# Turning normalised tokens by transposing transfers instead of float32 transposes on TensorE

## The chip, the cores and the metric

The kernel runs on one core of a Trainium2 chip. The metric is device time of one execution in microseconds (us); the kernel before takes 2276.16 us, the median of three runs (2273.22 to 2279.15).

## The reference

Two layers of a mixer over 2048 latent tokens and 256 context tokens, 1024 features each, float32. Cut to what matters here:

```python
h  = _rmsnorm(x, norm_g) * (1.0 + scale[:, None]) + shift[:, None]     # latents, modulated by c
hc = _rmsnorm(xc, norm_g) * (1.0 + scale_c) + shift_c                  # context, modulated by c_ctx
parts = _split_cols(h @ w_in)          # q, k, v, gates, and inputs of four mixers: 2816 columns
# Fourier mixing, attention over context + latents, short convolution, pooling, each gated by silu(z)
out = jnp.concatenate([o_f, o_att, o_c, o_p], axis=-1) @ w_out
x_new = x + gate[:, None] * out        # the context is updated likewise, in the first layer only
```

So each token's row is normalised, each feature multiplied by one factor and shifted by another, and the result is multiplied by the input weights.

## The kernel before, in words

Tokens are cut into five blocks (`BLK`): the context of 256 tokens and four latent blocks of 512; a tile is 128 tokens. The products with `w_in` need the tokens with features on the partitions. They are kept as a sum of two float16 numbers, so one block is four (context: two) tiles `h` of 4 KB per partition, and each product is done in three passes (`PASSES`).

`prep` (line 234) makes them, tile by tile, as a generator: it loads a tile of x token-major (one token per partition; the next tile's load is issued first), takes the sum of squares by a Square on ScalarE (L251, its elements go to a scratch), makes the scale from it on GpSimd (`rms_scale`, L230 and L231), and scales on ScalarE (L253); it yields; then it turns the tile by eight float32 transposes on TensorE (L261), applies factor and shift on VectorE from PSUM, where both are one number per partition (L265), casts to the high half on ScalarE (L268) and subtracts to the low half on GpSimd (L269).

`token_groups` (line 344) holds the products that come out token-major: per block two `fourier_in` (`tok_pair`, L329), one `keys` and one `values` (`tok_major`, L319) and two `queries` (L329). In layer 0 (lines 1147 to 1174) the preparation of the next block takes one step ahead of each group of the current block. In layer 1 (lines 1248 to 1266) two blocks are prepared first, among steps of the output projection of the last two blocks of layer 0 (`late`, L1125), and from then on preparation runs two blocks ahead, the context last. Feature-major groups (`feat_major`, L307) follow.

`big` hands out 26 shared buffers of 4 KB per partition: modulation weights, `h`, attention keys and values, output weights. `TagPool` holds buffers that a stage owns; `TOKEN` and the numbers beside it say how many. A scheduler places the instructions of each engine in a fixed order at build time, early in the program first; every engine then runs its own queue in order and waits on semaphores. Stores and most loads are on SP's queue, loads of `prep` on SP's for the first two blocks of layer 0 and otherwise on ScalarE's. `affine` (line 196) makes factor and shift with features on the partitions; `set_gate` (line 1080) spreads such a vector along the free axis over all partitions: a diagonal on VectorE, then a product with ones.

Of the kernel before, what the change touches and what calls it, by code (L numbers as in the profile page):

```python
# [10 lines left out]
F32 = mybir.dt.float32  # L11
F32R = mybir.dt.float32r
F16 = mybir.dt.float16
BF16 = mybir.dt.bfloat16
ACTF = mybir.ActivationFunctionType
ALU = mybir.AluOpType
# [4 lines left out]
D = 1024  # L21
KC = 8
# [4 lines left out]
BLK = [(0, 256)] + [(256 + 512 * i, 512) for i in range(4)]  # L27
# [15 lines left out]
def hybrid_kernel(ctx: ExitStack, tc: tile.TileContext, T, out):  # L43
    nc = tc.nc
    PE, ACT, DVE, POOL, SP = nc.tensor, nc.scalar, nc.vector, nc.gpsimd, nc.sync
# [9 lines left out]
    sm = pool("sm", 3)  # L55
# [15 lines left out]
    def big(shape, dt, name):  # L71
        return slot.tile(shape, dt, tag="s", name=name)
# [13 lines left out]
    id32 = const.tile([128, 128], F32, name="id32")  # L86
# [107 lines left out]
    aff = {}  # L194
# [23 lines left out]
    def alloc_h(b):  # L218
        n = BLK[b][1]
        per = 2048 // n  # L220
        hT[b] = [[big([128, per, n], F16, f"h{b}{part}{i}") for i in range(KC // per)] for part in range(2)]

    def h_ap(b, part, k, t0, n, nk=1):
        per = 2048 // BLK[b][1]
        t = hT[b][part][k // per]
        return t[:, k % per, t0:t0 + n] if nk == 1 else t[:, k % per:k % per + nk, t0:t0 + n]

    def rms_scale(ss, n, count, tag):
        ms = sm.tile([128, 8], F32, tag=tag, name=tag)[:, 0:n]
        POOL.tensor_scalar(out=ms, in0=ss, scalar1=1.0 / count, scalar2=EPS, op0=ALU.mult, op1=ALU.add)  # L230
        POOL.tensor_tensor(out=ms, in0=ms, in1=nh[:, 0:n], op=ALU.pow)  # L231
        return ms

    def prep(L, b, tp, psum):

        s = 1 if b == 0 else 0
        g0, n = BLK[b]

        def load(t):
            xt = tp.tile([128, D], F32, tag="x", name="xt")  # L240
            (SP if L == 0 and b < 2 else ACT).dma_start(out=xt, in_=source(L, g0 + t * 128))
            return xt

        ahead = load(0)
        for t in range(n // 128):
            xt = ahead
            if (t + 1) * 128 < n:
                ahead = load(t + 1)
            xn = tp.tile([128, D], F32, tag="xn", name="xn")
            ss = sm.tile([128, 1], F32, tag="ss", name="ss")  # L250
            ACT.activation(out=xn, in_=xt, func=ACTF.Square, accum_out=ss)  # L251
            rstd = rms_scale(ss, 1, D, "rx")
            ACT.activation(out=xn, in_=xt, func=ACTF.Copy, scale=rstd)  # L253
            yield
            if t == 0:
                alloc_h(b)
            for half in range(2):
                pt = psum()
                for j in range(4):
                    k = 4 * half + j  # L260
                    PE.transpose(out=pt[:, j * 128:(j + 1) * 128], in_=xn[:, k * 128:(k + 1) * 128], identity=id32)  # L261
                h32 = tp.tile([128, 4, 128], F32, tag="h32", name="h32")
                for j in range(4):
                    k = 4 * half + j
                    DVE.tensor_scalar(out=h32[:, j, :], in0=pt[:, j * 128:(j + 1) * 128], scalar1=aff[L][0][:, 0, k, s:s + 1],  # L265
                                      scalar2=aff[L][0][:, 1, k, s:s + 1], op0=ALU.mult, op1=ALU.add)
                hi = h_ap(b, 0, 4 * half, t * 128, 128, 4)
                ACT.copy(out=hi, in_=h32)  # L268
                POOL.tensor_tensor(out=h_ap(b, 1, 4 * half, t * 128, 128, 4), in0=h32, in1=hi, op=ALU.subtract)  # L269
# [821 lines left out]
    def source(L, tok):  # L1091

        if L > 0:
            return xd[tok:tok + 128]
        return T["ctx"][tok:tok + 128] if tok < NCTX else T["x"][tok - NCTX:tok - NCTX + 128]
# [50 lines left out]

    gate_w = {}
    with ExitStack() as st:
        tp = TagPool(st, tc, "s0", {**TOKEN, "x": 4, "xn": 2, "h32": 2, "row": 1})
        ws = []  # L1150
        ahead = prep(0, 0, tp, aux_bank)
        for c in range(4):
            for i, _ in enumerate(modulate(0, c, aux_bank, tp, True)):
                if (c, i) == (0, 3):
                    steps(ahead, 1)
                if (c, i) == (2, 3):
                    ws += [load_w(0, *TOKEN_W[0])]
        SP.dma_start(out=gain, in_=T["gains"].partition_broadcast(128))
        ws += [load_w(0, *TOKEN_W[1])]
        SP.dma_start(out=edge, in_=T["k_edge"])  # L1160
        SP.dma_start(out=invw, in_=T["k_invw"])
        SP.dma_start(out=cd, in_=T["k_cd"])
        affine(0)
        for w in ws:
            unscale(0, w[1])
        steps(ahead, 9)
        block = token_groups(0, tp, ws)
        for b in range(5):
            ahead = prep(0, b + 1, tp, aux_bank) if b + 1 < 5 else iter(())
            if b == 4:  # L1170
                gate_w[0] = load_w(0, *GATE_W[0:2], True)
            for _ in block(b):
                steps(ahead, 1)
            steps(ahead, 9)
# [26 lines left out]
    for L in range(DEPTH):  # L1201
# [37 lines left out]
        with ExitStack() as st:  # L1239
            tp = TagPool(st, tc, f"p{L}", {"mix": 1, "ml": 2, "ot": 1, "gate": 1, "x": 2})  # L1240
            project_setup(L, kvs)
            steps(att, 12)
            fill = project(L, early, tp)
            spread(att, fill, sum(72 if b else 11 for b in blocks[-2:]) - 12, sum(BLK[b][1] // 16 for b in early), 1)
            steps(fill, 1 << 30)
            steps(att, 1 << 30)
            right.close()
            late = project(L, blocks[-2:], tp)
            if L + 1 < DEPTH:
                with ExitStack() as st2:  # L1250
                    sp = TagPool(st2, tc, f"s{L + 1}", {**TOKEN, "s": 2, "x": 2, "xn": 1, "h32": 2}, "right")
                    with tc.issue_after(load_mark[0]):
                        block = token_groups(L + 1, sp, [])
                    for b in blocks[0:2]:
                        for _ in prep(L + 1, b, sp, mx_bank):
                            steps(late, 3)
                    for i, b in enumerate(blocks):
                        ahead = prep(L + 1, blocks[i + 2], sp, mx_bank) if i + 2 < 5 else iter(())
                        if i == 4:
                            gate_w[L + 1] = load_w(L + 1, *GATE_W[0:2], True)  # L1260
                        for _ in block(b):
                            steps(ahead, 1)
                            steps(late, 8)
                        steps(ahead, 9)
                        if i == 0:
                            steps(late, 1 << 30)
            steps(late, 1 << 30)
# [98 lines left out]
```

## Time and profile before

| | |
|---|---|
| median of three runs | 2276.16 us |
| the profiled execution, its own time | 2273.57 us |
| its span | 2271.8 us |
| TensorE busy | 2158.7 us, 95% |
| VectorE busy | 1407.4 us, 62% |
| ScalarE busy | 1227.9 us, 54% |
| GpSimd busy | 936.1 us, 41% |
| share of the chain that ended last on TensorE | 68% |
| transposes of `prep` (L261) | 288, first at 31.4, last at 1303.5 us |

The page cuts the span into 40 slices of 57 us; TensorE is at nine tenths or more in nearly all. Transposes of `prep` stand in slices 1 to 3 (layer 0) and 21 to 23 (layer 1) alone. A busy share is an average over a stretch; a wait is read from the timeline, where a line gives the start, the length, the engine, the program line, and in brackets the idle time before it and what ended it.

### The profile page before, as it was taken

The numbers are of one execution on the slowest core, as the hardware profiler recorded it, in microseconds if no ns is written. First come the engines' busy times: TensorE is split into PE (matmuls) and PEld (weight loads), VectorE is DVE, ScalarE is ACT, GpSimd is POOL, SyncE is SP. The second block draws the span as 40 slices with busy tenths as digits, with TensorE's granted clock in tenths as the row PEclk, the third lists the DMA queues.
The fourth block names the chain that finished last, engine by engine and source line by source line (L and its number), as shares of the span: only waits on it lengthen the run. The fifth ranks groups of instructions, "written<-read, shape, count | busy, mean of one in ns | idle before, by whom it ended". The sixth has DMA issues, their size and how long they took to land.

```text
span 2271.8 us, 41300 instructions
## 1 busy us (share of the span) xinstructions
PE 2158.7 (95%) x16327; PEld 1292.0 (57%) x16327; DVE 1407.4 (62%) x2639; ACT 1227.9 (54%) x2297; POOL 936.1 (41%) x996
## 2 busy tenths in 40 slices
PE   7999899989998999999999989999999999899999
PEld 3997556545555555545557984554454555455554
DVE  3655886366768767666465545413567776787743
ACT  4653454346777766544445624323467766566640
POOL 2786542215454455422125862011344556333320
PEclk9999999999999999999999999999999999999999
DMA  8424455510322110223474424323124210222133
GB/s 317 145 92 129 151 178 171 182 53 26 113 76 81 54 31 28 95 79 114 141 237 134 136 76 137 112 104 103 35 70 141 70 37 31 65 74 72 61 117 121
DMA packets 164081, 237.97 MB, mean 105 GB/s; under 512 B 28618, under 2 KB 113966, under 8 KB 163886
## 3 DMA queue, kind: packets, MB, share of 16 engines
q1 hardware_dynamic: 141294, 205.95, 27.2%
q10 hardware_dynamic: 22592, 29.37, 4.2%
q8 instruction: 128, 2.10, 0.4%
q14 instruction: 67, 0.55, 0.1%
HBM read 165.94 MB, written 69.34 MB: 104 GB/s over the span
## 4 chain that ended last, share of the span: by engine, by line
PE 68%; DVE 9%; ACT 4%; POOL 4%; issue 3%; DMA 2%; SPq 0%; POOLq 0%; DVEq 0%; ACTq 0%
PE fl L307 19%; PE fl L1125 15%; PE st L307 6%; PE pv L967 4%; PE st L972 4%; PE st L973 4%; PE mx L931 4%; DVE mp L932 2%; PE pv L965 2%; PE pv L329 1%; PE st L329 1%; PE mx L853 1%; DVE pl L979 1%; POOL pl L979 1%; PE mx L683 1%
## 5 line engine op out<-in xcount | busy, mean ns | idle before, releaser
L979 POOL TENSOR_TENSOR pl<-p,ph 128x512 f16<-128x512 f32 (+1 forms) x292 | 361.8, 1239 | 577.6 <-ACT p L978 515.1
L307 PE MATMUL fl<-h,w 128*128 128x512 f16 (+1 forms) x2592 | 582.1, 370 | 12.6 <-ACT w L147 9.3
L307 PEld LDWEIGHTS <-w 128*128 128x128 f16 x3456 | 331.5, 99 | 373.1 <-issue 22.2
L977 ACT ACTIVATE ph<-st 128x512 f16<-128x512 f32 (+1 forms) x584 | 350.9, 601 | 223.0 <-PE st L973 214.7
L932 DVE TENSOR_REDUCE mp<-mx 128x1 f32<-128x512 f32 (+1 forms) x648 | 388.8, 626 | 123.3 <-PE mx L931 112.7
L1125 PE MATMUL fl<-wo,ml 128*128 128x512 f16 x1632 | 376.8, 379 | 2.5 <-DVE ml L148 2.5
L978 ACT ACTIVATE p<-st 128x512 f32<-128x512 f32 (+1 forms) x584 | 351.2, 601 | 29.7 <-DVE pl L979 20.2
L979 DVE TENSOR_TENSOR pl<-p,ph 128x512 f16<-128x512 f32 (+1 forms) x292 | 231.9, 794 | 124.3 <-ACT p L978 100.0
L1125 PEld LDWEIGHTS <-ml 128*128 128x128 f16 x1632 | 157.4, 98 | 182.1 <-DVE ml L148 3.7
L967 PE MATMUL pv<-V,ph 128*128 128x130 f16 x2320 | 230.0, 221 | 6.9 <-ACT ph L977 6.2
L967 PEld LDWEIGHTS <-ph 128*128 128x128 f16 x2320 | 170.4, 98 | 116.4 <-ACT ph L977 29.1
L931 PE MATMUL mx<-kst,qhh 128*128 128x512 f16 x512 | 191.3, 385 | 22.9 <-DVE mp L932 22.1
L972 PE MATMUL st<-qhh,kst 128*128 128x512 f16 x512 | 195.6, 382 | 7.1 <-ACT p L978 6.2
L973 PE MATMUL st<-qlm,k 65*128 65x512 f16 x512 | 196.8, 384 | 0.0
L307 PE MATMUL st<-h,w 128*128 128x512 f16 (+1 forms) x864 | 189.1, 369 | 0.0
L965 PE MATMUL pv<-V,pl 128*128 128x66 f16 x2320 | 173.0, 194 | 12.5 <-DVE pl L979 6.0
L329 PEld LDWEIGHTS <-h 128*128 128x128 f16 x1632 | 160.0, 98 | 19.9 <-POOL h L269 1.1
L965 PEld LDWEIGHTS <-pl 128*128 128x128 f16 x2320 | 134.3, 98 | 65.0 <-POOL pl L979 14.0
L319 PEld LDWEIGHTS <-h 128*128 128x128 f16 x1728 | 99.5, 98 | 1.4 <-issue 0.6
L931 PEld LDWEIGHTS <-qhh 128*128 128x128 f16 x648 | 62.5, 99 | 65.8 <-issue 25.5
L329 PE MATMUL pv<-w,h 128*128 128x256 f16 x816 | 95.0, 275 | 0.9 <-POOL h L269 0.9
L329 PE MATMUL st<-w,h 128*128 128x256 f16 x816 | 92.7, 273 | 0.0
(303 smaller groups left out, 2903.7 us busy)
## 6 DMA issues: line engine op xcount, KB each, us to landing
wm<-in_w_mod_dram SPq DMA_DIRECT2D x48, 512.0 KB, 4.7
wst<-in_w_in_dram SPq DMA_DIRECT2D x44, 512.0 KB, 5.0
mix<-mixd SPq DMA_DIRECT2D x34, 512.0 KB, 4.0
zd<-z SPq DMA_DIRECT2D x64, 256.0 KB, 2.2
wst<-in_w_out_dram SPq DMA_DIRECT2D x32, 512.0 KB, 4.3
xt<-in_x_dram SPq DMA_DIRECT2D x20, 512.0 KB, 4.7
xd<-xt SPq DMA_DIRECT2D x18, 512.0 KB, 2.8
xt<-xd ACTq DMA_DIRECT2D x18, 512.0 KB, 3.7
```

Source lines behind the costliest of these rows:

```text
L307: PE.matmul(out=ps, lhsT=w[:, wp, k, :], rhs=h_ap(b, hp, k, 0, n), start=(k == 0 and i == 0), stop=(k == KC - 1 and i == 2))
L329: PE.matmul(out=ps[:, t], lhsT=h_ap(b, hp, k, (2 * i + t) * 128, 128), rhs=w[:, :, wp, k, :], start=(k == 0 and j == 0), stop=(k == KC - 1 ...
L931: mark[0] = PE.matmul(out=ps, lhsT=qhh[:, t * 128:(t + 1) * 128], rhs=kk, start=True, stop=True).ins
L932: DVE.tensor_reduce(out=mp[:, t, i:i + 1], in_=ps, axis=AX.X, op=ALU.max)
L965: PE.matmul(out=pv[t // 2][:, t % 2, 0:66], lhsT=p, rhs=v[:, 0:66], start=False, stop=(kt == nk - 1), skip_group_check=True)
L967: PE.matmul(out=pv[t // 2][:, t % 2, :], lhsT=p, rhs=v, start=(kt == 0 and t % 2 == 0), stop=False, skip_group_check=True)
L972: mark[0] = PE.matmul(out=ps, lhsT=self.k_tile(0, kt), rhs=qhh, start=True, stop=False).ins
L973: PE.matmul(out=ps, lhsT=self.k_tile(1, kt)[0:65, :], rhs=qlm[0:65, :], start=False, stop=True)
L977: ACT.activation(out=ph, in_=ps, func=ACTF.Exp, scale=1.0 / LOGIT)
L978: ACT.activation(out=p32, in_=ps, func=ACTF.Exp, scale=1.0 / LOGIT)
L979: (POOL if kt % 2 == 0 else DVE).tensor_tensor(out=pl, in0=p32, in1=ph, op=ALU.subtract)
L1125: PE.matmul(out=ps, lhsT=ml[:, mp, k, :], rhs=wo[k][:, wp, half * 512:(half + 1) * 512], start=(k == 0 and j == 0), stop=(k == KC - 1 and ...
```

## The change

For every block but the context of layer 0, `prep` hands over to a new generator. Factor and shift are spread along the free axis once for each layer and stream (`affine_rows`: two diagonals, four float32 products with ones, four copies, into shared buffers). A tile then stays token-major: Square into a float16 pair used as scratch, scale, one VectorE operation (times the token's scale, times the row of factors), one GpSimd addition (the row of shifts), one cast on ScalarE to the high half, one subtraction on VectorE to the low half; and each half is turned by transposing transfers on SP's queue straight into `h`, four per latent tile and two per context tile. The loads of layer 0's first latent block go to ScalarE's queue. The pair (`hl`) gets two buffers in each layer; in layer 1 it takes the place of `xn` and `h32`.

```diff
+    def affine_rows(L, s, psum):
+
+        for a in range(2):
+            dg = big([128, 8, 128], F32, "dg")
+            DVE.tensor_tensor(out=dg, in0=id32.unsqueeze(1).to_broadcast([128, 8, 128]),
+                              in1=aff[L][0][:, a, :, s].unsqueeze(2).to_broadcast([128, 8, 128]), op=ALU.mult)
+            r = big([128, 1024], F32, f"row{a}")
+            for half in range(2):
+                pg = psum()
+                PE.matmul(out=pg, lhsT=ones, rhs=dg[:, 4 * half:4 * half + 4, :].rearrange("p j f -> p (j f)"), start=True, stop=True)
+                ACT.copy(out=r[:, half * 512:(half + 1) * 512], in_=pg)
+            rows[a] = r
+
+    def prep_rows(L, b, tp, psum):
+
+        g0, n = BLK[b]
+        if b < 2:
+            affine_rows(L, 1 if b == 0 else 0, psum)
+
+        def load(t):
+            xt = tp.tile([128, D], F32, tag="x", name="xt")
+            ACT.dma_start(out=xt, in_=source(L, g0 + t * 128))
+            return xt
+
+        ahead = load(0)
+        for t in range(n // 128):
+            xt = ahead
+            if (t + 1) * 128 < n:
+                ahead = load(t + 1)
+            hl = tp.tile([128, 2, D], F16, tag="hl", name="hl")
+            ss = sm.tile([128, 1], F32, tag="ss", name="ss")
+            ACT.activation(out=hl.rearrange("p a f -> p (a f)").bitcast(F32), in_=xt, func=ACTF.Square, accum_out=ss)
+            rstd = rms_scale(ss, 1, D, "rx")
+            yield
+            if t == 0:
+                alloc_h(b)
+            DVE.scalar_tensor_tensor(out=xt, in0=xt, scalar=rstd, in1=rows[0], op0=ALU.mult, op1=ALU.mult)
+            POOL.tensor_tensor(out=xt, in0=xt, in1=rows[1], op=ALU.add)
+            ACT.copy(out=hl[:, 0], in_=xt)
+            DVE.tensor_tensor(out=hl[:, 1], in0=xt, in1=hl[:, 0], op=ALU.subtract)
+            per = 2048 // n
+            for part in range(2):
+                for i in range(KC // per):
+                    SP.dma_start_transpose(out=h_ap(b, part, per * i, t * 128, 128, per), in_=hl[:, part, per * 128 * i:per * 128 * (i + 1)])
+
     def prep(L, b, tp, psum):
 
+        if (L, b) != (0, 0):
+            yield from prep_rows(L, b, tp, psum)
+            return
...
-        tp = TagPool(st, tc, "s0", {**TOKEN, "x": 4, "xn": 2, "h32": 2, "row": 1})
+        tp = TagPool(st, tc, "s0", {**TOKEN, "x": 4, "xn": 2, "h32": 2, "hl": 2, "row": 1})
...
-                    sp = TagPool(st2, tc, f"s{L + 1}", {**TOKEN, "s": 2, "x": 2, "xn": 1, "h32": 2}, "right")
+                    sp = TagPool(st2, tc, f"s{L + 1}", {**TOKEN, "s": 2, "x": 2, "hl": 2}, "right")
```

## Rows read from the trace of the kernel before

**Rows 1.** Busy time by stretch: length, then busy us (instructions) per engine, clock, DMA

```profile
60.00:206.70 146.70, 146.70 (x1743) 137.41 (x1741) 81.56 (x193) 81.11 (x136) 114.69 (x140) 1.00 0.35 115
1225.00:1350.30 125.30, 124.96 (x1508) 117.03 (x1506) 70.18 (x174) 63.38 (x108) 99.02 (x118) 1.00 0.36 113
```

**Rows 2.** Timeline of TensorE in layer 1: start us, length us, line, operation

```profile
1188.92 1.88 PE L1087 MATMUL fl<-dg,ones 128*128 128x512 f32 x4
1190.64 0.67 PE L319 MATMUL pv<-w,h 128*128 128x128 f16 x9
...
1200.53 1.04 PE L261 MATMUL mx<-id,xn 128*128 128x128 f32 x8
1201.40 4.91 PE L1125 MATMUL fl<-wo,ml 128*128 128x512 f16 x22
```

**Rows 3.** Timeline, single moments of both token stages, several engines

```profile
41.02 0.23 DVE L212 TENSOR_SCALAR ab<-modT,sh 128x16 f32<-128x16 f32 x1
...
175.03 5.40 PE L329 MATMUL pv<-w,h 128*128 128x256 f16 x48
180.27 5.40 PE L329 MATMUL st<-w,h 128*128 128x256 f16 x48
...
206.71 0.28 PE L120 MATMUL mx<-sq,ones 128*128 128x2 f32 x2
...
1157.32 1.06 ACT L251 ACTIVATE xn<-xt 128x1024 f32<-128x1024 f32 x1 [3.17 <-PE mx L1015]
...
1352.99 2.84 PE L319 MATMUL st<-w,h 128*128 128x128 f16 x48
1355.67 0.34 PE L120 MATMUL mx<-sq,ones 128*128 128x2 f32 x2
```

**Rows 4.** Groups of instructions by line, whole span: count, busy us, mean ns, idle before

```profile
L174 DVE SCALAR_TENSOR_TENSOR acc<-wm,sc,acc 128x512 f32<-128x512 f32 x56 | 57.9, 1034 | 0.8
L979 DVE TENSOR_TENSOR pl<-p,ph 128x512 f16<-128x512 f32 (+1 forms) x292 | 231.9, 794 | 124.3 <-ACT p L978 100.0 <-PE pv L965 8.8 <-issue 6.2
L251 ACT ACTIVATE xn<-xt 128x1024 f32<-128x1024 f32 x36 | 38.0, 1056 | 48.3 <-PE mx L261 34.7 <-DMA xt<-in_ctx_dram 7.5 <-PE mx L1015 3.2
L251 ACT ACTIVATION_READ_ACCUMULATOR xn<-xt 128x1 f32 x36 | 6.8, 189 | 0.0
L231 POOL TENSOR_TENSOR rx<-rx,nh 128x1 f32<-128x1 f32 x36 | 21.2, 588 | 2.1
L230 POOL TENSOR_SCALAR rx<-ss 128x1 f32<-128x1 f32 x36 | 11.9, 330 | 51.3 <-ACT xn L251 49.9
L843 POOL TENSOR_TENSOR y<-y,zf 128x1024 f32<-128x1024 f32 x8 | 19.7, 2480 | 110.0 <-DVE y L832 110.0
L446 ACT CAST qo<-q 128x1024 f16<-128x1024 f32 x17 | 17.7, 1042 | 14.1 <-DVE q L426 13.2 <-DMA qd<-qo 1.0
L1082 DVE TENSOR_TENSOR dg<-id,modT 128x1024 f32<-128x1024 f32 x3 | 3.6, 1212 | 0.0
```

**Rows 5.** DMA issues (count, size, median us to landing), and one issue on SP's timeline

```profile
mix<-mixd SPq DMA_DIRECT2D x34, 512.0 KB, 4.0
gain<-in_gains_dram SPq DMA_DIRECT2D x1, 256.0 KB, 9.6
kd<-ko SPq DMA_DIRECT2D x2, 128.0 KB, 3.1
...
111.56 0.36 SPq L448 DMA_DIRECT2D qd<-qo  x1
```

**Rows 6.** Timeline: a quiet pair on VectorE early, then GpSimd and VectorE in layer 1

```profile
32.23 2.48 DVE L148 SCALAR_TENSOR_TENSOR w<-wst,ws,w 128x1024 f16<-128x1024 f32 x2 [0.58 <-ACT w L147]
...
1360.26 0.51 POOL L413 TENSOR_SCALAR rq<-rq,winv 128x4 f32<-128x4 f32 x2
...
1364.11 3.40 DVE L148 SCALAR_TENSOR_TENSOR w<-wst,ws,w 128x1024 f16<-128x1024 f32 x2 [0.95 <-ACT w L147]
...
1365.20 1.24 POOL L413 TENSOR_SCALAR rq<-rq,winv 128x4 f32<-128x4 f32 x1
```

More of the change, by code (lines that the diff above doesn't have):

```diff
@@ L232, in rms_scale @@
         return ms
+    rows = {}
+    def affine_rows(L, s, psum):
[37 more added lines that the diff above has]
+                    SP.dma_start_transpose(out=h_ap(b, part, per * i, t * 128, 128, per), in_=hl[:, part, per * 128 * i:per * 128 * (i + 1)])
     def prep(L, b, tp, psum):
+        if (L, b) != (0, 0):
+            yield from prep_rows(L, b, tp, psum)
+            return
         s = 1 if b == 0 else 0
@@ L240, in load @@
             xt = tp.tile([128, D], F32, tag="x", name="xt")
-            (SP if L == 0 and b < 2 else ACT).dma_start(out=xt, in_=source(L, g0 + t * 128))
+            SP.dma_start(out=xt, in_=source(L, g0 + t * 128))
             return xt
```

## The prediction

> **What bounds the kernel now.** I read the page's slices first: TensorE stands at nine tenths nearly everywhere. So the question is what TensorE does in the two stretches where normalised tokens are prepared, and what stands second there. The busy times by stretch answer that [rows 1]: from 60 us to the end of layer 0's token groups TensorE is busy for all 146.7 us of 146.7, GpSimd for 114.7 (78%), VectorE and ScalarE for 81 each (55%); in the later part of layer 1's token groups TensorE has 125.0 of 125.3 us, GpSimd 99.0 (79%). [...] So TensorE sets the pace, and a microsecond taken from it is worth a microsecond only as long as nothing else needs more than it leaves. The timeline gives the pace: the last block of layer 0, which prepares no tokens beside it, runs from 175.03 to 206.71, 31.7 us [rows 3]; a block that also turns four tiles of tokens needs 4 x 0.87 us more, 35.2 us.
>
> **What is taken from TensorE.** Eight float32 transposes of a tile stand in the queue for 0.87 us (1200.53 to 1201.40) [rows 2]. The change takes them from 34 of the 36 tiles (16 in layer 0, 18 in layer 1; the two context tiles of layer 0 keep the old way): 29.6 us.
>
> **What is put on TensorE.** The factors now vary along the free axis, so each stream needs two rows spread over all partitions: four float32 products of 512 columns, as the output gate already makes; two of those take 1.72 us (1188.92 to 1190.64) [rows 2], 0.86 each. Three sets (layer 0's latents, layer 1's latents and context): 12 x 0.86 = 10.3 us. Net on TensorE: 19.3 us less (10.5 in layer 0, 8.8 in layer 1). This is the largest gain the change can give.
>
> **What moves on the other engines, per tile** [rows 4]. ScalarE loses the scaled copy and gets one cast of 1.04 us for two half-size ones; it was 55% busy, and this is worth nothing by itself. VectorE loses eight small operations that read PSUM and gets two wide ones that read SBUF twice. The first, a scalar and two tensors over 1024 columns, lies between 1.24 us (half of the 2.48 us that the like weight split takes in quiet places, beside the 3.40 us for two in [rows 6]) and 2.07 us (twice the 1.03 us of the 512-wide accumulation); I take 1.5, near the weight split, which has the same width. The second, float32 minus float16 into float16, is twice 0.79 us: 1.6. GpSimd loses two subtractions and gets one addition of 1024 columns; the product of that shape takes 2.48 us: 2.5. The sums per tile change little. What changes is that these steps stand in a row. The diagonals (6 x 1.21 us on VectorE) and the row copies (12 on ScalarE of 512 columns, some 0.7 us each, between half and the whole of the 1.04 us of the cast twice as wide) come at the heads of the stages. The loads of block 1 move from SP's queue to ScalarE's, at about 0.35 us each on ScalarE: nothing, while its cover, ScalarE's idle half, lasts.
>
> **The transposing transfers.** No row shows one. Each tile has four of 128 KB on SP (two of 256 KB for a context tile). The lower bound is a plain transfer of 128 KB, issue to issue 0.36 us and 3.1 us to landing [rows 5]: 3 x 0.36 + 3.1 = 4.2 us for the four. The upper end is the slowest landing that the issue table shows, 9.6 us, with the four one after the other: 38 us. I take 6.5 us, 3 x 1.1 + 3.1, nearest to the mix load: it moves 1024 runs of 512 bytes in 4.0 us [rows 5], and a transposing transfer reads 512 runs of half that length, so about 1.1 us apart. Queued behind them on SP are the stores of u, keys and queries and the rope and weight loads; ScalarE's evacuations wait for those stores' buffers, and TensorE for ScalarE.
>
> [...]
>
> **Where a new wait arises.** The float16 pair (tag hl) has two buffers, and one is held from the Square, which scribbles into it, until its transfers have landed. Held time: Square 1.06 + 0.19, scale 0.33 + 0.59, multiply 1.5, add 2.5, cast 1.04, subtract 1.6, transfers 6.5, together 15.3 us [rows 4, 5]; plus six hand-overs to engines that are 55 to 79% busy with operations of about 1.2 us, at half an operation each: 3.9 us, an estimate. That is 19.2 us, and with two buffers one tile per 9.6 us. TensorE without transposes uses up a tile in 31.7 / 4 = 7.9 us. So the buffers, not TensorE, set the pace, and the wait sits in ScalarE's queue, ahead of PSUM evacuations. (Before, the like buffer came free when TensorE had turned the tile, a few microseconds after the Square.)
>
> Layer 0: the factors exist at 41.25 [rows 3]. One diagonal, two products and a copy bring the first row at 44.9, and the second at 46.6; then add, cast, subtract, transfers (2.5 + 1.04 + 1.6 + 6.5) and 3.4 of hand-overs: the first tile of block 1 lands at 61.7. The sixteenth lands 15 x 9.6 = 144 us later, at 205.7, and behind it block 4 still has its second u half, keys, values and queries, 26.4 us (180.27 to 206.71) [rows 3]: 232.1 against 206.7, a loss of 25.4 us.
>
> Layer 1: the first Square starts at 1157.3 [rows 3]; first tile at 1176.5, sixteenth at 1320.5, then 26.4 us and the context's keys and values (2 x 2.7): 1352.3 against the end at 1355.7 [rows 3], a gain of 3.4 us. Here preparation runs two blocks ahead and the rest of the output projection covers the slow start; TensorE alone would allow 1355.7 - 8.8 = 1346.9. The two x buffers, held until the subtraction now (4.0 us of load, like the mix load, and about 12 of chain), allow one tile per 8 us and don't bind first.
>
> The sum: +25.4 - 3.4 = +22 us on the profiled execution's own 2273.57 us, 2295.6; that execution lies 2.6 us under the median of the three runs, so 2298 on the median's scale.
>
> **The rivals.** (1) *All is hidden*: the held time stays under 15.8 us (hand-overs near nothing and transfers near the lower bound), TensorE keeps the pace, and the whole 19.3 us come: 2257. For it: layer 1 has slack, and the schedule can pull later work forward into gaps. Against it: the bare steps with the lower bound are already 13.0 us, and layer 0 prepares just one block ahead. (2) *Balance*: held time 16.8, a tile per 8.4 us: layer 0 loses 7.4 us (61.7 + 126 + 26.4 = 214.1), layer 1 gains its 8.8: 2275, no change.
>
> (3) *VectorE and GpSimd get in each other's way.* Where the weight split ran on VectorE, two for 3.40 us, a GpSimd operation that takes 0.26 us (two for 0.51) took 1.24 [rows 6]. The old preparation's VectorE work read PSUM; the new reads SBUF twice, beside GpSimd at 78%. If each of the two waits for a GpSimd operation and the addition for one of VectorE's, about 1 us each, the held time is 22.2 and the pace 11.1 us: layer 0 ends at 61.7 + 166.5 + 26.4 = 254.6 (+47.9), layer 1 at 1157.3 + 22.2 + 166.5 + 31.8 = 1377.8 (+22.1): 2346. This decides once the held time exceeds 19.2. [...]
>
> (4) *The transfers run in series* at 3.1 us each, 12.4 for the four: held 25.1, pace 12.6; layer 0 ends at 67.6 + 189 + 26.4 = 283.0 (+76.3), layer 1 at 1157.3 + 25.1 + 189 + 31.8 = 1403.2 (+47.5): 2400. The decisive point is whether one transfer's landing holds back the next. [...]
>
> **How the numbers follow.** Forecast 0.31 (2298), hidden 0.20 (2257), balance 0.12 (2275), interference 0.22 (2346), series 0.15 (2400). A measurement of this kernel tells 0.3%, 7 us, from no change; so faster 0.20, same 0.12, slower 0.68. The range runs from the hidden case with a few microseconds below it to the series case, 2253 to 2400; beyond it lie a slower series and a gain larger than TensorE's own, together under 0.2.
>
> **What the new profile would show.** Right: gaps on TensorE in the blocks of layer 0 that end on a transposing transfer, Squares that wait for those transfers, some 9 to 10 us between Squares, layer 0's token groups ending near 230 us and layer 1's unchanged within a few. Wrong: Squares 8 us apart or closer with TensorE full (hidden), VectorE's new operations at 2.5 us and more (interference), landings that follow one another at 3 us (series). A slot shortage among the 26 shared buffers, which the spread rows now use too, would also make it wrong; I priced it at nothing, since the most that I count at once in either token stage is 24.

## The result, and the profile after

The changed kernel takes 2344.16 us (median of four runs, 2341.82 to 2349.46) against 2275.85 us for the kernel before (median of four): a ratio of 1.0307, 95% interval 1.0284 to 1.0330, or 68 us more. The direction was as forecast, the size three times the forecast +22 us. The profiled execution of the changed kernel has a span of 2347.7 us, 75.9 us over the span before; it lies some 5 us above its own median, so the stages below add up to 76, not 68.

Line numbers of the changed kernel are those of before plus 50 behind the preparation. Its new lines: L240 diagonal (VectorE), L245 row product (TensorE), L246 row copy (ScalarE), L257 load, L267 Square, L272 multiply, L273 addition (GpSimd), L274 cast, L275 subtraction (VectorE), L279 transposing transfer (SP).

Busy times by stretch of the changed kernel: the token groups of layer 0, the end of layer 0's output projection, the token groups of layer 1. The columns are those of [rows 1]: TensorE, its weight loads, VectorE, ScalarE, GpSimd, clock, DMA share, GB/s.

```profile
55.50:248.80 193.30, 165.82 (x1766) 144.08 (x1767) 102.87 (x124) 74.86 (x124) 136.72 (x132) 0.92 0.65 145
1204.00:1244.10 40.10, 40.10 (x180) 18.45 (x179) 28.18 (x40) 18.71 (x24) 9.44 (x9) 1.00 0.64 215
1244.10:1419.20 175.10, 153.37 (x1618) 129.54 (x1617) 92.83 (x99) 65.57 (x106) 121.64 (x116) 0.96 0.71 167
```

TensorE, full before [rows 1], now idles 27.5 of 193.3 us in layer 0 and 21.7 of 175.1 in layer 1, and the granted clock falls with the gaps, to a mean of 0.92 and 0.96. In stretches of 2 us it stands at 1.00 or 0.50, but for those in which it changes: at 0.50 from 54 to 60 us, behind the gap ahead of the first product with normalised tokens. So a gap is paid twice: 12 products of 128x256 take 2.74 us there (from 56.74), 0.23 us each, where at 1.00 (62 to 78 us) 48 of them take 5.4, 0.11 us each. From layer 0's first product with normalised tokens to the end of its token groups TensorE is busy for 165.8 us, 6.9 more than before (158.9 of 159.8), though work was taken from it. The mean DMA share has about doubled, 0.65 and 0.71 against 0.35 and 0.36.

Who waits, and where, in layer 0. First ScalarE's start and TensorE's (timeline of the changed kernel: start us, length, engine, line; in brackets the idle time before and what ended it):

```profile
28.86 5.64 ACTq L257 DMA_DIRECT2D xt<-in_x_dram  x2
34.55 1.06 ACT L267 ACTIVATE hl<-xt 128x1024 f32<-128x1024 f32 x1 [15.56 <-DMA gain<-in_gains_dram]
35.60 1.04 ACT L333 ACTIVATE w<-wst 128x1024 bf16<-128x1024 f32 x1
...
37.88 0.56 PE L120 MATMUL mx<-sq,ones 128*128 128x2 f32 x2 [7.54 <-issue]
...
55.51 0.61 PE L379 MATMUL pv<-w,h 128*128 128x256 f16 x2 [2.97 <-ACT h L318]
```

Two loads of block 1 that were moved to ScalarE's queue didn't go out at once. The first is issued at 28.86, the second 5 us later, and ScalarE, whose next operation stands behind them in its queue, computes nothing for 15.56 us; the profile puts the end of that wait down to the landing of the gains. The weight Squares (L333) wait behind the loads, and the first product with normalised tokens comes at 55.5 instead of 46.9.

Then the first tiles of block 1: the rows, the addition, the first transfers, and TensorE's first wait for one (timeline, several engines):

```profile
64.11 0.58 ACT L246 COPY row<-fl 128x512 f32<-128x512 f32 x1
67.23 2.19 ACT L147 ACTIVATE w<-wst,ws 128x1024 f16<-128x1024 f32 x2 [2.55 <-DVE ws L143]
69.33 0.56 ACT L246 COPY row<-mx 128x512 f32<-128x512 f32 x1
...
72.24 5.57 POOL L273 TENSOR_TENSOR xt<-xt,row 128x1024 f32<-128x1024 f32 x2 [5.32 <-DVE xt L272]
...
76.60 6.65 SPq L279 DMA_TRANSPOSE h<-hl  x5
...
80.28 0.39 PE L379 MATMUL pv<-w,h 128*128 128x256 f16 x2 [2.42 <-DMA h<-hl]
```

Later the Squares wait for the pair that they scribble into (timeline of ScalarE):

```profile
87.30 1.06 ACT L267 ACTIVATE hl<-xt 128x1024 f32<-128x1024 f32 x1 [5.17 <-DMA h<-hl]
...
111.51 1.06 ACT L267 ACTIVATE hl<-xt 128x1024 f32<-128x1024 f32 x1 [5.24 <-DMA h<-hl]
...
207.22 1.06 ACT L267 ACTIVATE hl<-xt 128x1024 f32<-128x1024 f32 x1 [2.98 <-DMA h<-hl]
```

From the third Square (87.30) to the sixteenth (207.22) there are 13 steps: 9.2 us per tile.

In layer 1 the Squares wait in the same way. ScalarE at its start:

```profile
1207.56 1.04 ACT L267 ACTIVATE hl<-xt 128x1024 f32<-128x1024 f32 x1
...
1234.17 0.59 ACT L246 COPY row<-mx 128x512 f32<-128x512 f32 x1 [3.29 <-PE mx L245]
...
1248.56 1.06 ACT L267 ACTIVATE hl<-xt 128x1024 f32<-128x1024 f32 x1 [7.61 <-DMA h<-hl]
```

The row products stand in TensorE's queue behind the output projection, so the last row is copied at 1234 and the third Square starts 41 us after the second. What TensorE itself waits for here is another thing than in layer 0 (waits from 1200 us to 1420 us, and one of TensorE's timeline):

```profile
ACT hl L267 <- DMA h<-hl: 45.4, 16, 7.6
PE st L369 <- DVE r L472: 9.0, 3, 6.8
...
1345.56 1.99 PE L245 MATMUL mx<-dg,ones 128*128 128x512 f32 x4 [3.35 <-DVE dg L240]
```

ScalarE waits for the transfers, TensorE hardly at all (0.7 us). It waits for VectorE: 13.6 us in all for L472, the rotary product of keys and queries, which frees TensorE's output buffers, and 3.9 us for the diagonals of the context's rows. From 1248 on the chain of waits runs through the preparation. Its pieces in 1200 to 1425 us (start us, us, what), and ahead of them its sum by line:

```profile
by line: PE fl L1175 14.7%; DMA h<-hl 13.5%; POOL xt L273 10.1%; issue 7.2%; SPq L279 5.5%; POOL q L474 4.4%; POOL rq L231 3.7%; DVE xt L272 3.5%; POOL rx L231 3.3%; DVE hl L275 3.3%; DVE q L476 3.0%; DMA ud<-u 2.7%; ACT hl L274 2.7%; POOL 
...
1271.26 1.30 DVE xt L272
1272.62 3.29 POOL xt L273
1278.24 1.27 SPq L279
1280.86 4.24 DMA h<-hl
```

Transfers, the addition, SP's queue, the other preparation steps: no single one of them stands out. How the 76 us fall along the span is read from the ends of the token groups, where TensorE turns to the next work (timeline of TensorE, against [rows 3]):

```profile
248.84 0.28 PE L120 MATMUL mx<-sq,ones 128*128 128x2 f32 x2
...
1424.78 0.34 PE L120 MATMUL mx<-sq,ones 128*128 128x2 f32 x2
```

Layer 0's token groups end at 248.8 against 206.7 (+42.1, of which +8.6 had come by the first product); from there to layer 1's first Square (1206.50) it is 957.7 us against 950.6 (+7.1); from that Square to the end of layer 1's token groups 218.3 against 198.4 (+19.9); the rest +6.8.

### The profile page after: what moved, and what is told of

Its sections match the earlier page's. It is cut to its first block, busy times and chain, and to the rows that moved or that the text cites. A ratio compares the mean times of both kernels' runs of the same rounds, so it can differ in the third digit from the quotient of the medians.

```text
span 2347.7 us, 40730 instructions
## 1 busy us (share of the span) xinstructions
PE 2174.3 (93%) x16079; PEld 1281.2 (55%) x16079; DVE 1436.3 (61%) x2441; ACT 1193.3 (51%) x2241; POOL 965.1 (41%) x962
## 3 DMA queue, kind: packets, MB, share of 16 engines
q1 hardware_dynamic: 214574, 221.70, 31.2%
## 4 chain that ended last, share of the span: by engine, by line
PE 58%; DVE 9%; POOL 6%; ACT 6%; DMA 5%; issue 3%; SPq 1%; ACTq 0%; DVEq 0%; POOLq 0%
PE fl L357 17%; PE fl L1175 13%; PE st L357 5%; PE pv L1017 4%; PE mx L981 4%; PE st L1022 4%; PE st L1023 4%; PE pv L1015 2%; DVE mp L982 2%; DMA h<-hl 1%; PE mx L903 1%; DVE pl L1029 1%; POOL pl L1029 1%; ACT ph L1027 1%; POOL xt L273 1%
## 5 line engine op out<-in xcount | busy, mean ns | idle before, releaser
L379 PEld LDWEIGHTS <-h 128*128 128x128 f16 x1632 | 160.4, 100 | 60.5 <-DMA h<-hl 26.0
L379 PE MATMUL pv<-w,h 128*128 128x256 f16 x816 | 103.0, 285 | 19.7 <-DMA h<-hl 9.8
L369 PEld LDWEIGHTS <-h 128*128 128x128 f16 x1728 | 105.6, 102 | 14.4 <-issue 10.5
L273 POOL TENSOR_TENSOR xt<-xt,row 128x1024 f32<-128x1024 f32 x34 | 88.9, 2618 | 40.3 <-DVE xt L272 29.0
```

The source lines that it names most:

```text
L379: PE.matmul(out=ps[:, t], lhsT=h_ap(b, hp, k, (2 * i + t) * 128, 128), rhs=w[:, :, wp, k, :], start=(k == 0 and j == 0), stop=(k == KC - 1 ...
```

## The experiments

Each kernel ran in several rounds beside the kernel before; the medians of before were 2275.8 to 2277.2 us. "After" is 2344.2 us.

**One layer at a time.** `only_l0` prepares layer 1 in the old way, `only_l1` layer 0, each with the old buffers and loads there:

```diff
-        if (L, b) != (0, 0):
+        if L == 0 and b > 0:        # only_l0
+        if L == 1:                  # only_l1
```

> The change in layer 0 alone; layer 1 prepares its tokens as before. By the two traces' landmarks layer 0 carries about 42 us until its token groups end and 9 behind them, layer 1 some 18: expected 2320 to 2330. If layer 1's part is really the schedule's (what stands beside it in the order of the program), it is under 2316 or over 2340.

> The change in layer 1 alone; layer 0 prepares its tokens as before. Expected 2276 + 18 to 25, 2294 to 2301, if layer 1's loss stands by itself; 2276 or less if layer 1's loss comes from layer 0's later end (which moves what stands beside it).

`only_l0` took 2321.42 us (ratio 1.0194, interval 1.0176 to 1.0212), `only_l1` 2297.32 (1.0098, 1.0077 to 1.0118): 45 and 21 us over before, together 65 of the 68, both inside what was expected. The layers add up; both lose.

**The loads back on SP** (`loads_sp`):

```diff
-            ACT.dma_start(out=xt, in_=source(L, g0 + t * 128))
+            (SP if L == 0 and b < 2 else ACT).dma_start(out=xt, in_=source(L, g0 + t * 128))
```

> Only edit on the changed kernel: the loads of layer 0's first latent block go back to SP's queue. Theory S (the moved loads block ScalarE's queue at the start: the second Square idles 15.6 us there behind a load that waits, and the weight work behind it holds TensorE, whose first product with h starts at 55.5 instead of 46.9): about 10 us less, near 2334. Theory H (the float16 pair's two buffers set the pace) and theory X (the transposing transfers' issue and engine time set it): no change, 2344 within 4.

2328.90 us (1.0232, 1.0217 to 1.0247): 15 us less than after. The first product came at 45.6, earlier than before's 46.9, and ScalarE's weight Squares no longer waited (timeline of ScalarE in this kernel):

```profile
34.24 1.04 ACT L333 ACTIVATE w<-wst 128x1024 bf16<-128x1024 f32 x1
...
35.28 1.04 ACT L333 ACTIVATE w<-wst 128x1024 bf16<-128x1024 f32 x1
```

So the moved loads cost 15 us.

**More pairs** (`pair4_l0`: in layer 0 the pair shares the tag and the four buffers of xn; layer 1 keeps two):

```diff
-            hl = tp.tile([128, 2, D], F16, tag="hl", name="hl")
+            hl = tp.tile([128, 2, D], F16, tag="xn", name="hl")
-        ... "xn": 2, "h32": 2, "hl": 2, "row": 1}
+        ... "xn": 4, "h32": 2, "row": 1}
```

> Only edit on the changed kernel: in layer 0 the float16 pair shares the four buffers of the context's xn, so that four pairs may be held after the context; layer 1 keeps two. Theory H: layer 0's token groups lose most of the 33 us that they gained after the first product, 20 to 30 us less, 2315 to 2325, and the waits of the Square for the transfers go away in layer 0. Theory X: SP and the DMA engines stay as loaded, the transfers only queue up, 2344 within 7. Theory S: no change.

2333.27 us (1.0256, 1.0237 to 1.0274): 11 us less, about half of the least that theory H wanted. The pairs are one limit among others.

**A shorter hold** (`sq_slot`: the Square writes a scratch tile of its own, the pair is taken just ahead of the cast):

```diff
-            ACT.activation(out=hl.rearrange("p a f -> p (a f)").bitcast(F32), in_=xt, ...)
+            sqt = big([128, D], BF16, "sqt")
+            ACT.activation(out=sqt, in_=xt, ...)
```

> Only edit on the changed kernel: the Square writes its unused elements to a shared buffer of its own (bfloat16), and the pair is taken just before the cast, so that it is held some 9 us (cast, subtract, transfers) instead of 16 to 20. Theory H: 25 to 45 us less in both layers together, 2300 to 2320. Theory X: under 10 us less. In layer 1 the two x buffers become the next limit, which may keep half of its share.

2336.09 us (1.0262, 1.0244 to 1.0280): 8 us less, a miss for H. (The scratch tile takes one of the 26 shared buffers; no run shows what that costs.)

**The addition on VectorE** (`add_dve`):

```diff
-            POOL.tensor_tensor(out=xt, in0=xt, in1=rows[1], op=ALU.add)
+            DVE.tensor_tensor(out=xt, in0=xt, in1=rows[1], op=ALU.add)
```

> Only edit on the changed kernel: the addition of the row of shifts runs on VectorE instead of GpSimd. After the first runs gave back 7 to 15 us each for the transfers' kind, the pair's number and its hold, theory P: a tile's chain and the rotary chain of queries and keys share GpSimd's queue in order (79% busy before), and the 2.6 us addition in the middle of the tile's chain, with ScalarE's cast and the evacuations behind it, is what spaces the tiles. P expects 25 to 40 us less (2304 to 2319), since 41 us of GpSimd in each layer's token stage become some 24 us of VectorE, which is half idle. Theory X with H (transfers and their buffers): within 10 us of 2344.

2334.99 us (1.0258, 1.0236 to 1.0280): 9 us less, a miss for the size that P wanted.

**The turn left out** (`plain`: the same bytes between the same tiles by plain transfers, so the tokens reach TensorE unturned):

```diff
-                    SP.dma_start_transpose(out=h_ap(b, part, per * i, t * 128, 128, per), in_=hl[...])
+                    SP.dma_start(out=h_ap(b, part, per * i, t * 128, 128, per), in_=hl[...].rearrange("p (k f) -> p k f", f=128))
```

> On the changed kernel, the 132 transposing transfers are plain copies of the same bytes between the same buffers on the same queue; the turn itself is left out, so the products are of tokens that are not turned. Theory X: without 1.25 us of issue each on SP and with less time on the DMA engines, 30 to 45 us less, 2300 to 2315. Theory H: the pair is held some 5 us less, a tile per 6 us, which also gives most of the pace back: 20 to 40 us less. If neither holds and the longer chain at the start and the rows are the cost, under 10 us less.

2337.54 us (1.0270, 1.0249 to 1.0291): 7 us less, a miss. By itself none of the suspects is worth more than 15 us.

**Three edits at once** (`add_dve_sp_pair4`: `loads_sp`, `pair4_l0` and `add_dve` together):

> Three edits on the changed kernel together: addition on VectorE, first loads back on SP, four pairs in layer 0. If the parts add up: the sum of their single gains, 15 + 11 and what the addition gives by theory P (25 to 40), so 2280 to 2295. If they are the same gaps seen from three sides: about the best of the three alone, 2310 to 2329.

2314.20 us (1.0170, 1.0151 to 1.0188): 30 us less, against 35 for the sum of the three. The time lies in the range that stood for "the same gaps seen from three sides", but that range had counted on 25 to 40 us from the addition, which alone gave 9; by the single gains as measured, the three costs are nearly separate. What holds the other 37 us was open; the kernels built on this one, whose names end in `_r8`, asked for it.

**Block 1 in the old way** (`old_block1`: float32 transposes for layer 0's block 1, the rows from block 2 on. As it was run, layer 1's context block was given the latents' rows, so one set of four row products and its copies is left out):

```diff
-        if (L, b) != (0, 0):
+        if L == 1 or b > 1:
-        if b < 2:
-            affine_rows(L, 1 if b == 0 else 0, psum)
+        if b == 2 - L:
+            affine_rows(L, 0, psum)
```

> The three edits together (add_dve_sp_pair4), and block 1 of layer 0 prepared in the old way: float32 transposes on TensorE, no rows, loads on SP; the rows and the new way begin with block 2, in layer 1 all is new. What is left in layer 0 after the three edits is 173.7 us from the first product with h to the last of the token groups, against 159.7 before. Theory B: it is the start of block 1, whose first tile has no work to hide its chain (rows, addition, split, transfer). Then the stage falls to 150 to 158 us, since blocks 2 to 4 have TensorE work ahead of them: 2294 to 2300 in all. Theory X (the transposing transfers, whose engines are full in 75 to 165 us, limit every block): the stage stays above 168: 2308 to 2316.

2316.36 us (1.0182, 1.0163 to 1.0201): no gain, and layer 0's stage stays at 173 us; theory B falls. The gap that block 1 had in 75 to 105 us had only moved to where the transfers now began. Busy times by stretch, `add_dve_sp_pair4` first, then `old_block1`:

```profile
75.00:105.00 30.00, 16.73 (x184) 14.63 (x185) 14.65 (x14) 8.09 (x13) 10.19 (x13) 0.83 1.00 176
105.00:135.00 30.00, 30.00 (x323) 27.51 (x322) 24.78 (x28) 15.71 (x27) 20.97 (x24) 0.95 1.14 215
```

```profile
75.00:105.00 30.00, 30.00 (x360) 27.13 (x358) 22.51 (x24) 11.12 (x18) 14.36 (x12) 1.00 0.51 98
105.00:135.00 30.00, 23.46 (x256) 20.02 (x254) 18.96 (x22) 13.09 (x22) 17.45 (x21) 0.89 1.10 177
```

The column before the last is the DMA share: in both kernels the stretch with the gap is the one in which it first reaches 1.0 or more. The share alone doesn't make the gap: at 1.14, in the first kernel's next stretch, TensorE is full.

**Layer 1's rows early** (`rows_early_r8`: `affine_rows` for layer 1 is called behind `project_setup`. As in `old_block1`, the context's own rows are left out, so the run does four products less than the "same work" of the expectation):

> The three edits together, and layer 1's rows of gain and shift are built ahead of the layer's output projection, not at the first tile of its block 1 (same work, 4 float32 products, 4 row copies). Theory R: the first tile of layer 1 waits for the rows (11 us of the addition's waits in the changed kernel were for the row copy), so the token stretch of layer 1 falls from 174.5 to 164 to 168 us: 2303 to 2308. If the rows only wait beside other work: 2311 to 2317.

2314.15 us (1.0161, 1.0142 to 1.0181): no gain. In layer 1 the first transfer started 12 us earlier (1193.59 against 1205.60), and yet the token groups ended at 1387 against 1383 (416.6 against 417.7 us after the output projection's first product). Building the latents' rows early gives nothing once the three edits are in.

**A shorter hold on top** (`sq_slot_r8`):

> The three edits together, and the Square writes a scratch tile of its own, so that a pair is held from the cast on and not from the load on. Layer 1 still has two pairs. Theory H (the hold of the pairs sets layer 1's token stretch, 174.5 us): 6 to 12 us less there, 2302 to 2308. If the transfers or the rows set it: 2311 to 2317.

2316.71 us (1.0177, 1.0152 to 1.0201): no gain; an earlier release of the pairs no longer counts.

**The turn left out, on top** (`plain_r8`: the edit of `plain` on the three edits):

> The three edits together, and each transposing transfer replaced by a plain transfer of the same bytes between the same tiles; the turn is left out. Theory X: with the other waits lifted, the turn itself is what is left in both layers: layer 0 loses 8 us or more of its 173.7 and layer 1 another 8 of its 174.5 (alone, plain took 9 us off layer 1's token stretch): 2294 to 2300. Theory B (block 1's chain, of which the transfer is one link of five): 2306 to 2313, layer 1 giving most of it.

2284.73 us (1.0039, 1.0024 to 1.0055): 29.5 us less than `add_dve_sp_pair4`. What alone was worth 7 us is worth four times that once the other waits are gone. So most of the rest of the loss is in the transfers' being transposing ones. But which of their properties? The transfers in `add_dve_sp_pair4`, then in `plain_r8` (engine, operation, count: length of the issue in ns, least, median, most; then the time to landing in us):

```profile
L279 SPq DMA_TRANSPOSE h<-hl x132: 1188/1257/2811, 69.0 to 1352.6; - x132
...
DMA to landing us min/median/max: 2.4/4.1/13.0
```

```profile
L279 SPq DMA_DIRECT2D h<-hl x132: 593/630/1732, 68.7 to 1326.4; - x132
...
DMA to landing us min/median/max: 2.3/4.4/8.4
```

The landing takes no longer, 4.1 us at the median against 4.4. The issue holds SP's queue twice as long, 1.26 us against 0.63, and the transfers of that queue take more of the 16 engines' time (queue, packets, MB, share; 45 to 220 us, the same two kernels):

```profile
q1 hardware_dynamic: 44064, 19.67, 55.2%
```

```profile
q1 hardware_dynamic: 44128, 21.37, 43.4%
```

**Issue time without the turn.** `plain_half_r8` cuts each plain transfer of `plain_r8` into two, `plain_split_r8` into pieces of 128 columns (four; eight for a context tile); bytes and places are the same:

```diff
-                    SP.dma_start(out=h_ap(b, part, per * i, t * 128, 128, per), in_=...)
+                    for k in range(0, per, per // 2):
+                        SP.dma_start(out=h_ap(b, part, per * i + k, t * 128, 128, per // 2), in_=...)
```

> The three edits together, with plain transfers (the turn is left out), each of them cut into four of 32 KB: the same bytes between the same places, in four times as many issues. In plain_r8 a plain transfer of 128 KB takes SP's queue 0.63 us, a transposing one 1.25 us; four small ones take at least 4 times 0.36 us = 1.4 us. Theory Q (what the transposing transfers cost is the time that they hold SP's queue, with the stores and loads behind them): the 29 us that plain_r8 gained fall away again, 2305 to 2325. Theory E (it is the time on the 16 DMA engines, 52.6 to 55.2% of a token stage on that queue against 42.6 to 43.4% for plain ones): 2282 to 2292, as plain_r8.

> The three edits together, with plain transfers (the turn is left out), each cut into two of 64 KB: by plain_split_r8's 0.60 us for an issue of 32 KB and plain_r8's 0.63 us for one of 128 KB, two of them hold SP's queue 1.25 us for 128 KB, as long as one transposing transfer does, with the engines' work of plain ones. Theory Q (the hold of SP's queue is all of the 29 us): 2308 to 2320, as add_dve_sp_pair4. Theory E (the engines' time is): 2283 to 2292, as plain_r8. Between: both, in the measure of where it falls.

`plain_split_r8` took 2434.25 us (1.0699, 1.0681 to 1.0717), `plain_half_r8` 2297.78 (1.0101, 1.0083 to 1.0120). Their issues, in the same order:

```profile
L280 SPq DMA_DIRECT2D h<-hl x544: 464/599/1710, 67.7 to 1484.6; - x182
```

```profile
L280 SPq DMA_DIRECT2D h<-hl x264: 593/619/1613, 68.3 to 1342.2; - x132
```

An issue costs some 0.6 us whether it carries 32, 64 or 128 KB, so the quarters came out far beyond both ranges, which had counted on 0.36. Counted over the kernel by these medians, SP's queue is held 132 x 0.63 = 83 us by the plain transfers, 264 x 0.62 = 163 by the halves, 132 x 1.26 = 166 by the transposing ones, 544 x 0.60 = 326 by the quarters; the times are 2285, 2298, 2314 and 2434. The quarters show what the queue alone can do. Their stretch of layer 0, and SP in it:

```profile
135.00:165.00 30.00, 17.22 (x115) 10.91 (x116) 12.53 (x16) 7.95 (x12) 9.04 (x12) 0.64 0.39 102
...
139.68 11.58 SPq L280 DMA_DIRECT2D h<-hl  x16
...
151.99 11.41 SPq L280 DMA_DIRECT2D h<-hl  x16
```

TensorE is busy 17 of 30 us, every other engine less than half, the DMA engines 39%, while SP has one tile's transfers behind the other: SP is late. The halves match the transposing transfers in issue time and not in the turn: with them 13 of the 29.5 us gained are lost again. So 13 us (some 5 either way, by the intervals) are SP's queue; the other 16 are what is left by subtraction, with the DMA engines' time as the likeliest place (the share of that queue was 40.4% with the halves, 55.2% with the turn). That no run separates further.

**Two issuing engines** (`two_queues_r8`: the low halves are issued by ScalarE):

```diff
-                    SP.dma_start_transpose(out=...)
+                    (SP, ACT)[part].dma_start_transpose(out=...)
```

> The three edits together, and of each tile's four transposing transfers the two of the low halves are issued by ScalarE, the others by SP as before; nothing is left out. SP's queue is held 2.5 us less per tile, ScalarE's queue 2.5 us more (ScalarE is busy 16 of 30 us in layer 0's token stage). Theory Q: 2295 to 2307. Theory E: the engines have the same work, 2310 to 2320. If ScalarE's queue, with the copies, Squares and loads in it, becomes the one that is late: 2320 to 2340.

2395.31 us (1.0523, 1.0508 to 1.0539), far outside all of it. The first eight of SP (timeline of SP):

```profile
69.31 28.90 SPq L279 DMA_TRANSPOSE h<-hl  x8
```

Eight transfers of 1.2 us of issue each take 28.9 us. The first four go out in a row; from 76.28 on one of ScalarE and one of SP alternate, each issued when the other has landed (chain of waits, landings):

```profile
76.28 4.29 DMA h<-hl
...
80.62 2.41 DMA h<-hl
```

Eight such turns take until 99.43, 2.9 us each, where one queue issues a transfer every 1.25 us; SP waits up to 5.99 us at a time, and ScalarE's own work stands still behind its share, 17.5 us the first time. The waits are semaphore waits in the two queues: the program as built takes turns, and what the chip would do without them the run doesn't show. So the run tells nothing of Q against E.

**SP's stores elsewhere** (`stores_off_r8`: ud, the store of u, from ScalarE; kd and qd, those of keys and queries, from GpSimd):

```diff
-            SP.dma_start(out=ud[...], ...)
+            ACT.dma_start(out=ud[...], ...)
-            SP.dma_start(out=kd[...], ...)
+            POOL.dma_start(out=kd[...], ...)
-            SP.dma_start(out=qd[...], ...)
+            POOL.dma_start(out=qd[...], ...)
```

> The three edits together, nothing left out, and the token stages' stores no longer on SP: ud is issued by ScalarE, which wrote it, kd and qd by GpSimd, which wrote them. SP's queue then holds the transposing transfers, the rope tables and the weights, and doesn't wait for ScalarE's u or GpSimd's ko and qo (some 38 us of SP's waits in 60 to 220 us, 25 us in 1208 to 1390). Theory Q with the waits in front of the transfers: 2295 to 2306. If only the issues' own time counts (8 stores of 0.37 us in a block): 2308 to 2314. If GpSimd's issue of a store delays its own work: slower than 2316.

2322.37 us (1.0198, 1.0181 to 1.0216): 8 us slower. SP's waits for u, ko and qo are gone, but other waits take their place ahead of the transfers (SP's queue, 60 to 225 us: total us, times, longest):

```profile
SPq L441 <- DVE r L472: 31.2, 5, 10.1
...
SPq L279 <- ACT hl L274: 8.7, 3, 4.3
```

The rope table's load waits 31.2 us for VectorE's r, 3.2 in `add_dve_sp_pair4`. The waits in front of the transfers move, they aren't a price by themselves. Whether GpSimd's own work was delayed by its stores, which the expectation gave as the reason for a time above 2316, the run doesn't separate.

## Why the prediction was wrong in size

By the runs the 68 us are 30 for the three edits, 29.5 for the transposing transfers once these are in, and 8.6 that no run took away. The steps of the prediction that failed are two: the start of each stage, which was summed as if every queue were free and the moved loads cost nothing, and the transfers, which were priced as latency alone.

**TensorE's gain** of 19.3 us never came as time. With the turn left out and three waits lifted (`plain_r8`) the kernel still stands 8.6 us above before, which makes some 28 us to find. By the same moments as above, `plain_r8`'s profiled execution loses 1.0 us to the end of layer 0's token groups, where TensorE was to gain 10.5, and 4.0 in layer 1's, where it was to gain 8.8; 6.1 come behind them. The largest single wait of TensorE in these stages is one that the sum had at nothing. The context's row products were priced at their own length, but they stand in order in TensorE's queue and wait there for a diagonal from VectorE (timeline of TensorE in `plain_r8`):

```profile
1290.82 3.78 PE L245 MATMUL mx<-dg,ones 128*128 128x512 f32 x4 [8.82 <-DVE dg L240]
```

The changed kernel has 3.9 us of such waits in layer 1, `add_dve_sp_pair4` 11.8. Lifting them is not shown to pay: `old_block1` and `rows_early_r8` leave the context's rows out, and TensorE waits for the rotary product (L472) there instead.

**The loads of block 1** were priced at "nothing, while its cover, ScalarE's idle half, lasts". This step failed outright: 15 us. What was counted was 0.35 us of issue each. The loads also held up what stood behind them in ScalarE's queue: it idles for 15.56 us with the weight Squares in line. "Half idle" is a mean over the stage, and this was the head of the stage.

**The first tile** was put at 61.7 us in layer 0 and 19.2 us after the first Square in layer 1. The first transfer was issued at 76.60, and TensorE's waits for that tile's transfers end at 80.28 and 84.04, 22 us late. In layer 1 the third Square, which needs the first tile's pair back, came 42 us after the first, where the sum had 19.2 to the landing. In layer 0 this is the term that carries the error of the sum: the end was forecast at 232.1 and came at 248.8. The chain was summed as if every queue were free at its turn. In layer 0 the row copies stood behind a weight split, the last at 70.27; in layer 1 the row products stood behind the projection, the last copy at 1234. Part of it were the moved loads (`loads_sp`, 15 us of the kernel's time). For the rest `rows_early_r8` and `old_block1` show that an earlier start gives nothing by itself while the transfers limit.

**The pace** was forecast at 9.6 us per tile from a held time of 19.2, and came at 9.2. The step held, and its experiment still fell short: four pairs gave 11 us and an early release 8, where the step makes the pair the only limit. The reading that fits is that several limits lay at nearly the same pace, and that with the pairs freed the transfers took over; no run takes away these two alone together.

**The transfers** are the mis-sized term. The four of a tile were put at 6.5 us as latency in the chain. By the measured medians they need 3 x 1.25 + 3.6 = 7.4 us, with the issue from this view of the changed kernel and the median landing under it:

```profile
L279 SPq DMA_TRANSPOSE h<-hl x132: 1188/1252/2395, 76.6 to 1393.7; - x132
...
DMA to landing us min/median/max: 2.4/3.6/6.6
```

Near enough. But four of them also hold SP 5.0 us of every 9.2, and the prediction named the stores and loads behind them and gave that no price. Nor did it add the engines' work, though the DMA share of before stood in [rows 1]. In the runs that is 29.5 us once the other waits are gone, 13 of them SP's queue. Series landings, rival (4), didn't happen: the issues follow each other at 1.25 us while each takes 3.6 to land. Beside plain transfers between the same tiles (`add_dve_sp_pair4` against `plain_r8`) the transposing ones were as fast in the landing, 4.1 against 4.4 us, and not in the issue, 1.26 against 0.63 us, nor in the time of the kernel, 2314 against 2285 us.

**Interference**, rival (3), gave about the size that came (2346), by luck: its mechanism is not what the runs show. Groups by line of the changed kernel:

```profile
L272 DVE SCALAR_TENSOR_TENSOR xt<-xt,rx,row 128x1024 f32<-128x1024 f32 x34 | 50.9, 1502 | 61.6 <-POOL rx L231 48.2 <-ACT hl L274 13.4
L275 DVE TENSOR_TENSOR hl<-xt,hl 128x1024 f16<-128x1024 f32 x34 | 46.0, 1354 | 43.2 <-ACT hl L274 39.9 <-DMA h<-hl 3.2
...
L273 POOL TENSOR_TENSOR xt<-xt,row 128x1024 f32<-128x1024 f32 x34 | 88.9, 2618 | 40.3 <-DVE xt L272 29.0
```

The multiply took 1.50 us in the mean, as sized (median 1.29), the subtraction 1.35 (1.22), the addition 2.62 where 2.5 was put (2.35): 0.6 us a tile over the medians, not the 3 us of that rival. Some additions did take 3.3 us beside VectorE (the chain above; VectorE's addition L1182, 0.69 us at the median, took 2.13 beside that one, from 1274.31), so the interference shows, at a fraction of its price.

**Layer 1** was to gain 3.4 us, since "the rest of the output projection covers the slow start". The projection did keep TensorE busy (40.10 of 40.10 us up to 1244), and the loss came behind it, 21.7 us of gaps in the token groups, most of them for VectorE's rotary product. The prediction looked for the wait in ScalarE's queue alone. Of the two in-between losses, +7.1 and +6.8 us, the timeline accounts for some 3: ScalarE's weight split behind layer 1's token groups made TensorE wait 12.3 us in place of 8.1 + 1.2. The rest is open.

## What to carry to other kernels

Before work goes from a full engine to a transfer queue, sum what the queue itself will hold (issues x their length, per unit of the loop) and what stands behind it in order: here 5.0 us of every 9.2, priced as latency alone. Where several limits lie at nearly the same pace, lifting one shows little (7 to 15 us each here) until the others are gone (29.5 us for the one that alone gave 7), so take them away together before clearing a suspect. A load moved to a computing engine's queue is priced by what waits behind it at the moment of the move (here 15.56 us of idle ScalarE, and 15 us of the kernel's time), not by the engine's mean idle share.

## What the runs showed of the hardware

- An issue of SP between two tiles in SBUF takes about 0.6 us for 32, 64 or 128 KB (`plain_split_r8`, `plain_half_r8`, `plain_r8`), and 1.25 us for a transposing one of 128 KB. Size doesn't show here either: the four transposing transfers of 256 KB for the context, the last of layer 1, took 1.24 to 1.29 us each in the changed kernel.
- Some four times as many issues for the same bytes cost 150 us (2285 to 2434), with the DMA engines at 39% in the stretch shown.
- Transposing transfers issued by two engines in turn, each waiting on a semaphore for the other's landing, took 2.9 us each (76.28 to 99.43 for eight); one queue alone issued one every 1.25 us (changed kernel, median).
- Gaps on TensorE went with a lower clock: in layer 0's token groups the mean granted clock (1.00 or 0.50 in stretches of 2 us, but for those in which it changes) fell from 0.98 to 0.92 as TensorE's idle time rose from 0.9 of 159.8 to 27.5 of 193.3 us, and its busy time rose by 6.9 us.
